# A hybrid encoder layer on one core: the mLSTM's backward pass copies its keys on DVE, loads its first decays earlier, and 36 projection products change place

## The chip, the cores and the metric

The kernel runs on one core of one Trainium2 chip. The metric is the device time of one execution in microseconds (us): the median of the runs of a kernel. Engines are named as in the profile: PE (TensorE), DVE (VectorE), ACT (ScalarE), POOL (GpSimd), SP (SyncE, which issues nearly all DMAs here).

## The reference, cut to what matters

One layer of a Hymba-style encoder over 2048 tokens of width 1024, in float32. After a modulated RMSNorm, one input projection feeds two groups of heads: eight attention heads of width 64 with two key/value heads in a band of 128 tokens, and four mLSTM heads of width 128, which scan the sequence forward and backward. Both groups are normalised, joined, projected and gated; a SwiGLU feed-forward layer and a last RMSNorm follow. The mLSTM of one head and direction, in chunks of 128 tokens:

```python
w = jnp.exp(a - a_max[..., None])
kv_c = jnp.einsum('bchs,bchsk,bchsv->bchkv', w, kc, vc)        # keys x weighted values, per chunk
c_new = decay[..., None, None] * c_st + inj[..., None, None] * kv   # state, chunk after chunk
sc = jnp.einsum('bchtd,bchsd->bchts', qc, kc) * dw              # scores in the chunk, with decays dw
num = (jnp.einsum('bchts,bchsv->bchtv', sc, vc)
       + inter[..., None] * jnp.einsum('bchtk,bchkv->bchtv', qc, c_prev))
hout = num / jnp.maximum(jnp.abs(den), jnp.exp(-m_t))[..., None]
```

Queries and keys of the mLSTM come from the projection through a convolution over three tokens and SiLU.

## The kernel before, in words

The order of PE's instructions is written out by hand for the whole kernel. In the mLSTM stage (from some 190 us to 572 us of the span) DVE, ACT, POOL and SP run in the order in which the code issues their work as well; from the attention on those four are ordered by a scheduler. PE works through the stage in order, so a product whose operand is late holds all that follows.

**Filler products.** Projection tiles are written as generators in the list `fill`; `pull(n)` issues the next n matmuls (`gps`, L607, 128x128 by 128x512, 96 for a tile of 128 columns by 2048 tokens, 24 for one block of 512). `at_step` runs between them what is due: a tile's weights are loaded (`wraw`, L257) and split in a high part on ACT (`whi`, L261) and a low part on POOL (`wlo`, L267), stores in `dues` are issued on SP (L296), and work in `posts` is run. After a block of a convolution tile ACT evicts it (L636, `edge` L637), DVE adds the neighbours (L641 and L642), later ACT takes the tanh (L622) and DVE multiplies (L625). While head h of the mLSTM runs, the tiles of the next head's queries and keys are its filler (768 products in all), and in the last head `first`, four tiles of attention keys and queries (384). The numbers of products in each place (`nb`, `nf`, `pull(5)`, `pull(36)`) are set by hand.

**One head of the mLSTM (`mlstm`)** has a backward pass over its 16 chunks, 15 to 0, and a forward pass. A chunk of the backward pass begins with `tick()`, which runs the work in `later` that is due. Then `k_chunk` transposes the chunk's keys on PE (`ktp`, L735, in PSUM bank a), copies them to SBUF (`kn`, L737, ACT), and scales the values (`vw`, L740, ACT). One chunk later PE multiplies the two (`kvp`, L745), and DVE brings the state on (`cb`, L766 for the first, L769 for the others). The sixteen `kn` of a head are kept, and the forward pass uses them again, except that of chunk 0, which it makes itself. `kvp` lies in banks c, d, c, b in turn. Keys and values are loaded in blocks of four chunks (`mqk`, `mv`); block 0 of queries, keys and values for the forward pass, and the decays `bc` of its first three chunks (L726), are loaded when the backward pass is at chunk 2.

The forward pass begins with `decays` (POOL, `ng`, L785), `scaled_q` (POOL, `qs`) and `exps` (ACT, L797). For each chunk PE then makes `sps` (L806, in banks d and b in turn), and for the chunk before it `kvp` (in bank a), and `num` (L836 and L838). DVE divides (`rd`, `hst`).

**The norm of a head** comes when its forward pass is over, so for heads 0 to 2 inside the next head's backward pass: 12 small instructions of DVE for the reciprocal square roots (L100 to L107), POOL scales four blocks (L867, `hst`), and `store` transposes each block on PE (`htp`, L872, bank a), scales it on ACT (`og`, L874, one buffer) and stores it by SP (L875, at the next tick). Blocks follow each other three ticks apart. Head 3's blocks are normalised one by one, the last in the tail: eight times a tick and `pull(5)`.

**The attention** starts with its loads `aq`, `ak`, `av` (L906 to L910), which read what `first` has stored, then `pull(36)` of its own filler (the tile `second` and the output-gate tiles), and the first scores `as` (L926). Its filler has 480 products; what the attention leaves of them is done at its end, around the start of the output projection (799 to 827 us).

Of the kernel before, what the change touches and what calls it, by code (L numbers as in the profile page):

```python
# [16 lines left out]
AF = mybir.ActivationFunctionType  # L17
# [5 lines left out]
P = 128  # L23
# [7 lines left out]
HM = 4  # L31
# [6 lines left out]
def hybrid_layer_kernel(  # L38
# [5 lines left out]
    pe, dve, act, pool, sp = nc.tensor, nc.vector, nc.scalar, nc.gpsimd, nc.sync  # L44
# [8 lines left out]
    def bank(tag, name):  # L53
        return pp.tile([P, 512], F32, tag=tag, name=name, bufs={"g": 2, "a": 2, "b": 1, "c": 2, "d": 1}[tag])
# [13 lines left out]
    mxm_d = dp.tile([HM, NT, P, P], F32, name="mxm_d")  # L68
# [43 lines left out]
    def pull(n=1):  # L112

        while n > 0 and fill:
            if next(fill[0], None) is None:
                fill.popleft()
            else:
                n -= 1

    def finish_fill(g):  # L120
        while any(f is g for f in fill):
            pull()
# [573 lines left out]
    later = []  # L696

    def tick():

        due = [f for k, f in later if k <= 0]  # L700
        later[:] = [[k - 1, f] for k, f in later if k > 0]
        for f in due:
            f()

    def load_v(h, n):
        va = s2.tile([P, 4, 129], F32, tag="mv", name="mv", bufs=2)
        sp.dma_start(va, vaug_d[n * 512:(n + 1) * 512, h, :].rearrange("(c p) d -> p c d", p=P))
        return va

    def load_qk(h, j, n):  # L710
        t = s2.tile([P, 512], F32, tag="mqk", name="mqk", bufs=4)
        sp.dma_start(t, qk_d[j, h, n])
        return t

    def load_last(h):
        return load_qk(h, 1, NB - 1), load_v(h, NB - 1)

    def mlstm(h, nb, nf, last):
# [5 lines left out]
        def load_bc(cc):  # L724
            bc = s2.tile([P, 4, P], F32, tag="bc", name="bc", bufs=3)
            sp.dma_start(bc.rearrange("p j t -> p (j t)"), bc_d[h, cc].rearrange("j t -> (j t)").partition_broadcast(P))  # L726
            return bc
# [3 lines left out]
        def k_chunk(k_c, va_c, d, cc):  # L731
            kn = kns.get(cc)
            if kn is None:
                tp = bank("a", "ktp")
                pe.transpose(tp[:, :P], k_c, ident)  # L735
                kn = kns[cc] = s2.tile([P, P], F32, tag=f"kn{cc}", name="kn", bufs=1)
                act.activation(kn, tp[:, :P], AF.Copy)  # L737
            vw = s2.tile([P, 129], F32, tag="vw", name="vw", bufs=3)
            rr = row(d, cc)
            act.activation(vw, va_c, AF.Copy, scale=wT[:, rr:rr + 1])  # L740
            return kn, vw

        def kv_mm(kn, vw, tag="a"):
            kvp = bank(tag, "kvp")
            pe.matmul(kvp[:, :129], kn, vw, start=True, stop=True)  # L745
            return kvp


        blk = {}
        todo = deque()  # L750
        blk[NB - 1] = last
        for cc in list(range(NT - 1, 0, -1)) + [0, 0]:
            tick()
            n, i = divmod(cc, 4)
            if i == 3 and n:
                blk[n - 1] = (load_qk(h, 1, n - 1), load_v(h, n - 1))
            if cc == 2:
                ahead = (load_qk(h, 0, 0), load_qk(h, 1, 0), load_v(h, 0)), [load_bc(i) for i in range(3)]
            if cc:
                todo.append((cc, *k_chunk(blk[n][0][:, i * P:(i + 1) * P], blk[n][1][:, i, :], 1, cc)))  # L760
                pull(nb - nb // 2)
            if len(todo) > 1 or (todo and not cc):
                c_, kn, vw = todo.popleft()
                kvp = kv_mm(kn, vw, "bcdc"[c_ % len("bcdc")])
                if c_ == NT - 1:
                    dve.tensor_copy(cb[:, c_ - 1, :], kvp[:, :129])  # L766
                else:
                    rr = row(1, c_)
                    dve.scalar_tensor_tensor(cb[:, c_ - 1, :], cb[:, c_, :], dec[:, rr:rr + 1], kvp[:, :129], MUL, ADD)  # L769
                pull(nb // 2)  # L770


        blk = {0: ahead[0]}
        out_ = []
        ssq = s2.tile([P, NT], F32, tag="mssq", name="mssq")
        ends = {NT - 1: 0} if h < HM - 1 else {4 * n + 3: n for n in range(NB)}
        bcs = dict(enumerate(ahead[1]))
        ngs, qss = {}, {}
        cf = None
        todo = None  # L780
# [18 lines left out]
        def scores(cc):  # L799
            n, i = divmod(cc, 4)  # L800
            if cc + 1 < NT:
                decays(cc + 1)
            qt, kt, va = blk[n]
            q_c, k_c, va_c = qt[:, i * P:(i + 1) * P], kt[:, i * P:(i + 1) * P], va[:, i, :]
            s = bank("db"[cc % 2], "sps")
            pe.matmul(s[:, :P], k_c, q_c, start=True, stop=True)  # L806
            kv = k_chunk(k_c, va_c, 0, cc) if cc < NT - 1 else None
            sc = s2.tile([P, 2, P], F32, tag="sc", name="sc")
            dve.scalar_tensor_tensor(sc, s[:, :P].unsqueeze(1).to_broadcast([P, 2, P]), DS, ngs.pop(cc), MUL, MUL)
            return cc, sc, va_c, kv  # L810
# [48 lines left out]
        def norm(n0, n):  # L859

            r = rsqrt(s2, ssq[:, 4 * n0:4 * n + 4], 4 * (n + 1 - n0), P, f"mr{n - n0}")
            for j in range(n0, n + 1):
                later.append([j - n0, partial(scale, j, r[:, 4 * (j - n0):4 * (j - n0) + 4])])
                later.append([3 * (j - n0) + 3, partial(store, j, out_[j])])
# [2 lines left out]
            pool.tensor_tensor(out_[j], out_[j], r.unsqueeze(2).to_broadcast([P, 4, P]), MUL)  # L867

        def store(n, hst):
            tp = bank("a", "htp")  # L870
            for i in range(4):
                pe.transpose(tp[:, i * P:(i + 1) * P], hst[:, i, :], ident)  # L872
            og = s2.tile([P, 512], F32, tag="og", name="og", bufs=1)
            act.activation(og, tp, AF.Copy, scale=gml[:, h:h + 1])  # L874
            later.append([0, lambda: sp.dma_start(mxm_d[h, 4 * n:4 * n + 4].rearrange("c p t -> p c t"),  # L875
                                                  og.rearrange("p (c t) -> p c t", c=4))])

        decays(0)
# [22 lines left out]
    def att_loads(bi, kv):  # L901
        k0, k1 = max(0, bi - 1), min(NT - 1, bi + 1)
        nk = k1 - k0 + 1
        ks = slice(k0 * P, (k1 + 1) * P)
        q = s3.tile([P, 4, P], F32R, tag="aq", name="aq")
        sp.dma_start(q.bitcast(F32), qst_d[kv * 4:kv * 4 + 4, :, bi * P:(bi + 1) * P].rearrange("h p t -> p h t"))  # L906
        kk = s3.tile([P, 2, 3 * P], F32R, tag="ak", name="ak")
        sp.dma_start(kk[:, :, :nk * P].bitcast(F32), kst_d[kv, :, :, ks].rearrange("z p t -> p z t"))
        v = s3.tile([P, 3, P], F32R, tag="av", name="av", bufs=4)
        sp.dma_start(v[:, :nk, :].bitcast(F32), vst_d[ks, kv].rearrange("(n p) z d -> p n (z d)", p=P))  # L910
        return bi, kv, nk, (k0 - bi + 1) * P, q, kk, v
# [211 lines left out]
    for i in range(2 * 96 + 60):  # L1123
# [8 lines left out]
        elif i == 226:  # L1132
            last = load_last(0)
# [5 lines left out]
    for h in range(HM):  # L1139
        if h:  # L1140
            for g in convs[h]:
                finish_fill(g)
            last = load_last(h)
            pull(45)
        mlstm(h, 3, 9, last)
    for _ in range(8):
        tick()
        pull(5)
    for g in first:
        finish_fill(g)  # L1150
    while posts:
# [148 lines left out]
    chain0 = first_pair(nxt)  # L1300
    order = [(bi, kv) for kv in range(KV) for bi in range(NT)]
    ahead = deque(att_loads(*o) for o in order[:2])
    pull(36)
    u1 = u2 = None
    for s_ in range(len(order) + 2):
        if s_ + 1 == NT:
# [414 lines left out]
    with tc.tile_pool(name="ff", bufs=1, side="right", reuse_waits="tile") as ff:  # L1721
# [203 lines left out]
        def operands(u, k):  # L1925
            if u == "A11":
                load_w2(W11, k)
            if u == "S2":
                load_w2(W22, k)
            a = load_a(u, k)  # L1930
            w = op_w(u, k)
            if u == "A11" :
                load_w2(W12, k)
            return a, w
# [106 lines left out]
        for u in ("A11", "S2", "S3", "A22", "S1", "S4", "A12"):  # L2041
# [11 lines left out]
            for k in range(KH - KL):  # L2053
                a, w = early.pop(0) if early else operands(u, k)
# [44 lines left out]
```

## Time and profile before

| | |
|---|---|
| median of 3 runs | 2274.69 us (2273.98 to 2275.52) |
| profiled execution | 2283.18 us, of which span 2281.4 us |
| PE busy | 2228.5 us, 98% of the span, 10968 matmuls |
| DVE, ACT, POOL busy | 1590.8 us, 1058.4 us, 1049.6 us |
| head 1: backward pass | about 318.5 to 338.3 us |
| head 2: backward pass | about 405 to 424 us |
| head 3: backward pass | about 492 to 510.5 us |
| start of the attention | from 571.7 us; its first scores at 587.31 us |

The profile is of one execution, whose own time is above the median of the runs. Times in rows are microseconds from the start of the span. In a row of the timeline the brackets at the end give how long the engine was idle before it, and what it then waited for. A row with x2 or more stands for as many instructions in a run, and its duration for all of them.

### The profile page before, as it was taken

What the parts mean: (1) busy time and instruction counts of PE and PEld (TensorE: products, weight loads), DVE (VectorE), ACT (ScalarE), POOL (GpSimd) and SP (SyncE); (2) the same over time, 40 slices, a digit from 0 to 9 for tenths busy, and PEclk for the clock granted to TensorE, in tenths of its full rate; (3) what the DMA queues carried; (4) which work ended last, traced back from release to release, by engine and by line L of the source; (5) the groups of instructions that cost most, each with busy time, mean ns of one, the idle gap of its engine ahead of it and who ended that gap; (6) DMA issues with size and microseconds to landing.
All of it is one profiled execution on the core that took longest, in us unless ns stands there. A gap on an engine that the chain in (4) does not pass through costs nothing.

```text
span 2281.4 us, 32599 instructions
## 1 busy us (share of the span) xinstructions
PE 2228.5 (98%) x10968; PEld 1875.9 (82%) x10968; DVE 1590.8 (70%) x2788; ACT 1058.4 (46%) x2204; POOL 1049.6 (46%) x909
## 2 busy tenths in 40 slices
PE   8999999999899999999999999999999999999998
PEld 8897878888788878778888888788888888888887
DVE  6876667546687887786767686776766666785694
ACT  5424655544577756354544443533333333233452
POOL 0007424425334434536656666456666655592020
PEclk9999999999999999999999999999999999999999
DMA  9667744776666576763343453533333373543462
GB/s 344 222 197 234 226 150 149 221 210 198 195 178 192 173 238 212 267 222 134 111 171 111 145 185 128 193 102 102 106 100 108 99 280 130 165 153 93 147 213 93
DMA packets 355500, 393.41 MB, mean 172 GB/s; under 512 B 21388, under 2 KB 253180, under 8 KB 355332
## 3 DMA queue, kind: packets, MB, share of 16 engines
q1 hardware_dynamic: 355108, 391.28, 52.6%
q8 instruction: 87, 1.43, 0.3%
q14 instruction: 81, 0.66, 0.1%
q10 hardware_dynamic: 224, 0.04, 0.0%
HBM read 272.05 MB, written 119.19 MB: 171 GB/s over the span
## 4 chain that ended last, share of the span: by engine, by line
PE 54%; DVE 2%; ACT 1%; DMA 1%; issue 1%; SPq 0%; ACTq 0%
PE fp L1747 36%; PE fo L59 5%; PE fo L58 5%; PE fo L57 5%; PE ops L57 1%; PE ops L59 1%; PE ops L58 1%; DVE al L1865 1%; DVE ra L2007 1%; DVE w L1874 0%; DMA al<-a_d 0%; ACT T L1561 0%; PE trn L167 0%; DMA A22r<-in_w_ffn_in_dram 0%; DVE ra L2023 0%
## 5 line engine op out<-in xcount | busy, mean ns | idle before, releaser
L607 PE MATMUL gps<-hT,whi 128*128 128x512 f32 x1088 | 398.4, 420 | 0.3 <-DVE cacc L642 0.3
L1747 PE MATMUL fp<-T,S 128*128 128x512 f32 x1584 | 368.9, 390 | 0.3 <-DVE T L1562 0.3
L1747 PEld LDWEIGHTS fp<-T,S 128*128 128x128 f32 x1584 | 296.4, 188 | 62.4 <-DVE T L1562 1.0
L1747 PE MATMUL fp<-B,A 128*128 128x512 f32 x1056 | 246.5, 389 | 0.0
L59 PE MATMUL fo<-w,al 128*128 128x512 f32 x616 | 239.8, 389 | 0.5 <-DVE al L1865 0.5
L58 PE MATMUL fo<-w,ah 128*128 128x512 f32 x616 | 239.7, 389 | 0.0
L57 PE MATMUL fo<-w,ah 128*128 128x512 f32 x616 | 239.7, 389 | 0.0
L1747 PEld LDWEIGHTS fp<-B,A 128*128 128x128 f32 x1056 | 198.2, 188 | 41.2
L607 PE MATMUL gps<-hT,wlo 128*128 128x512 f32 x544 | 227.7, 418 | 0.0
L607 PEld LDWEIGHTS gps<-hT,whi 128*128 128x128 f32 x1088 | 201.6, 191 | 24.0 <-DVE cacc L642 0.7
L1865 DVE TENSOR_TENSOR al<-al,ah 128x1024 fp32r<-128x1024 f32 x77 | 116.3, 1515 | 110.7 <-ACT ah L1864 110.1
L1864 ACT ACTIVATE ah<-al 128x1024 fp32r<-128x1024 f32 x77 | 81.6, 1060 | 183.5 <-DMA al<-a_d 182.2
L1597 DVE TENSOR_TENSOR S<-sf,S 128x512 fp32r<-128x512 f32 x86 | 132.4, 1577 | 30.0 <-ACT S L1596 29.9
L1597 DVE TENSOR_TENSOR A<-graw,A 128x512 fp32r<-128x512 f32 x86 | 132.7, 1565 | 11.2 <-ACT A L1596 11.1
L1767 DVE SCALAR_TENSOR_TENSOR g<-t,g 128x512 f32<-128x512 f32 x44 | 45.2, 1026 | 135.4 <-ACT t L1766 135.4
L59 PEld LDWEIGHTS fo<-w,al 128*128 128x128 f32 x616 | 115.6, 188 | 24.9 <-DVE al L1865 1.0
L58 PEld LDWEIGHTS fo<-w,ah 128*128 128x128 f32 x616 | 115.6, 188 | 24.2
L57 PEld LDWEIGHTS fo<-w,ah 128*128 128x128 f32 x616 | 115.6, 188 | 24.2 <-ACT ah L1864 0.2
L1747 PE MATMUL fp<-T,A 128*128 128x512 f32 x528 | 129.4, 394 | 2.1 <-ACT u L1773 2.1
L942 POOL TENSOR_SCALAR ap<-ap,adn 128x384 f32<-128x384 f32 (+1 forms) x128 | 73.0, 590 | 124.2 <-DVE adn L940 40.9
L1747 PE MATMUL fp<-B,S 128*128 128x512 f32 x528 | 127.0, 389 | 1.8 <-ACT c L1770 1.8
L1601 POOL TENSOR_TENSOR sf<-A,A22r 128x512 f32<-128x512 f32 x43 | 59.6, 1387 | 147.4 <-DMA A22r<-in_w_ffn_in_dram 104.0
(424 smaller groups left out, 5237.4 us busy)
## 6 DMA issues: line engine op xcount, KB each, us to landing
al<-a_d SPq DMA_DIRECT2D x77, 512.0 KB, 5.0
wmod<-in_w_mod_dram SPq DMA_DIRECT2D x48, 512.0 KB, 7.0
graw<-in_w_ffn_in_dram SPq DMA_DIRECT2D x43, 512.0 KB, 3.8
a_d<-ka SPq DMA_DIRECT2D x66, 256.0 KB, 4.5
bc<-bc_d SPq DMA_DIRECT2D x64, 256.0 KB, 4.7
hop_d<-n SPq DMA_DIRECT2D x56, 256.0 KB, 4.9
a_d<-u SPq DMA_DIRECT2D x55, 256.0 KB, 4.5
mqk<-qk_d SPq DMA_DIRECT2D x48, 256.0 KB, 4.1
```

Of the source, the lines that this page charges most:

```text
L57: pe.matmul(o, lh, rh, start=first, stop=False, skip_group_check=skip)
L58: pe.matmul(o, lh, rl, start=False, stop=False, skip_group_check=skip)
L59: pe.matmul(o, ll, rh, start=False, stop=last, skip_group_check=skip)
L607: pe.matmul(ps, w[i == 2][:, k, :], hT[n](i == 1, k), start=(k == 0 and i == 0), stop=(k == KT - 1 and i == 2))
L942: pool.tensor_scalar(self.p[g][:, :self.NK], self.p[g][:, :self.NK], dn[:, g:g + 1], 0.0, MUL, ADD)
L1597: dve.tensor_tensor(t[:, 1, :], f, t[:, 0, :].bitcast(F32), SUB)
L1601: pool.tensor_tensor(f1, a21, a22, ADD)
L1747: pe.matmul(ps, w[:, s, k * P:(k + 1) * P], f[k // 2][:, k % 2, :], start=first and n_ == 0, stop=n_ == 11, skip_group_check=True)
L1767: dve.scalar_tensor_tensor(g0, t0, 1.0, g0, ADD, MUL)
L1864: act.activation(ah, al.bitcast(F32), AF.Copy)
L1865: dve.tensor_tensor(al, al.bitcast(F32), ah.bitcast(F32), SUB)
L2007: dve.tensor_tensor(ra[i], ra[i], xr, ADD)
```

## The change

- In the backward pass the copy of the transposed keys, `kn`, is made by DVE in place of ACT (15 a head; the copy for chunk 0 in the forward pass stays on ACT).
- The decays of the first three chunks are loaded at chunk 8 of the backward pass, not at chunk 2; block 0 of the queries at chunk 5. Block 0 of keys and values is no longer loaded again for the forward pass: the buffers of the backward pass are used.
- The backward pass's `kvp` lie in banks c, d, c in turn (by the chunk's number modulo 3). The transposes `htp` of the results lie in bank b, except for head 3. The store of `og` is issued one tick later.
- The last head's forward pass pulls one filler product fewer at each of its 16 steps (nf 8 for 9), each of the eight steps of the tail 4 in place of 5, and 56 in place of 36 are pulled ahead of the attention's first scores. No product is added or dropped.

```diff
@@ k_chunk
-                act.activation(kn, tp[:, :P], AF.Copy)
+                if d:
+                    dve.tensor_copy(kn, tp[:, :P])
+                else:
+                    act.activation(kn, tp[:, :P], AF.Copy)
@@ mlstm, backward pass
-            if cc == 2:
-                ahead = (load_qk(h, 0, 0), load_qk(h, 1, 0), load_v(h, 0)), [load_bc(i) for i in range(3)]
+            if cc == 8:
+                bcs = {i: load_bc(i) for i in range(3)}
+            if cc == 5:
+                q0 = load_qk(h, 0, 0)
...
-                kvp = kv_mm(kn, vw, "bcdc"[c_ % len("bcdc")])
+                kvp = kv_mm(kn, vw, "cdc"[c_ % 3])
...
-        blk = {0: ahead[0]}
+        blk = {0: (q0, *blk[0])}
...
-        bcs = dict(enumerate(ahead[1]))
@@ store
-            tp = bank("a", "htp")
+            tp = bank("b" if h < HM - 1 else "a", "htp")
...
-            later.append([0, lambda: sp.dma_start(mxm_d[h, 4 * n:4 * n + 4].rearrange("c p t -> p c t"),
+            later.append([1, lambda: sp.dma_start(mxm_d[h, 4 * n:4 * n + 4].rearrange("c p t -> p c t"),
@@ the heads, the tail, the attention
-        mlstm(h, 3, 9, last)
+        mlstm(h, 3, 9 if h < HM - 1 else 8, last)
     for _ in range(8):
         tick()
-        pull(5)
+        pull(4)
...
-    pull(36)
+    pull(56)
```

## Rows read from the trace of the kernel before

**Rows 1.** The page, first part: busy time, share of the span, instructions.
```profile
PE 2228.5 (98%) x10968; PEld 1875.9 (82%) x10968; DVE 1590.8 (70%) x2788; ACT 1058.4 (46%) x2204; POOL 1049.6 (46%) x909
```

**Rows 2.** Waits of PE, 230 to 660 us: us in total, times, longest.
```profile
PE kvp L745 <- ACT vw L740: 7.3, 8, 2.3
...
PE ktp L735 <- ACT og L874: 2.3, 3, 1.3
...
PE sps L806 <- DVE cb L769: 0.5, 1, 0.5
```

**Rows 3.** Windows: length, busy PE, PEld, DVE, ACT, POOL, granted clock, DMA, GB/s.
```profile
200.00:220.00 20.00, 20.00 (x90) 16.57 (x89) 1.00 0.85 284
...
430.00:433.00 3.00, 3.00 (x9) 2.41 (x8) 2.86 (x10) 2.70 (x10) 1.40 (x2) 0.50 0.97 296
586.60:593.40 6.80, 6.09 (x18) 5.18 (x19) 3.01 (x13) 2.50 (x9) 0.92 (x3) 0.50 0.79 241
799.00:827.00 28.00, 26.73 (x124) 21.92 (x123) 23.69 (x45) 15.02 (x20) 9.96 (x8) 1.00 0.89 296
```

**Rows 4.** Timeline at the turns of heads 1, 2 and 3: start, us, instruction.
```profile
335.70 0.50 SPq L726 DMA_DIRECT2D bc<-bc_d  x1
...
341.20 0.74 POOL L785 TENSOR_TENSOR ng<-bc,maskb 128x256 f32<-128x256 f32 x1 [13.93 <-DMA bc<-bc_d]
...
343.17 0.49 PE L745 MATMUL kvp<-vw,kn 128*128 128x129 f32 x2 [1.33 <-ACT vw L740]
...
428.19 0.49 PE L745 MATMUL kvp<-vw,kn 128*128 128x129 f32 x2 [2.05 <-ACT vw L740]
...
515.73 0.49 PE L745 MATMUL kvp<-vw,kn 128*128 128x129 f32 x2 [2.26 <-ACT vw L740]
```

**Rows 5.** Instructions by form: ns least/median/most, first and last start.
```profile
L737 ACT ACTIVATE kn<-ktp x64: 252/277/287, 236.0 to 515.1; 128x128 f32<-128x128 f32 x64
L766 DVE COPY cb<-kvp x4: 278/288/292, 237.4 to 492.3; 128x129 f32<-128x129 f32 x4
L625 DVE SCALAR_TENSOR_TENSOR cacc<-ctanh,cacc x32: 679/692/1783, 193.6 to 433.4; 128x512 f32<-128x512 f32 x32
```

**Rows 6.** Timeline of DVE, then PE, start of head 1's backward pass.
```profile
320.00 0.16 DVE L100 TENSOR_SCALAR mr3v<-mssq 128x16 f32<-128x16 f32 x1
...
322.08 0.17 DVE L107 SCALAR_TENSOR_TENSOR mr3y<-mr3a,mr3y 128x16 f32<-128x16 f32 x1
...
322.38 3.00 DVE L625 SCALAR_TENSOR_TENSOR cacc<-ctanh,cacc 128x512 f32<-128x512 f32 x2
...
323.43 0.38 PE L745 MATMUL kvp<-vw,kn 128*128 128x129 f32 x2
```

**Rows 7.** Timeline of PE, start of head 3's backward pass.
```profile
490.69 0.28 PE L735 MATMUL ktp<-ident,mqk 128*128 128x128 f32 x1
...
492.87 0.38 PE L745 MATMUL kvp<-vw,kn 128*128 128x129 f32 x2
```

**Rows 8.** Timeline: head 2's start on DVE; head 1's turn on PE, DVE.
```profile
406.29 0.75 DVE L641 SCALAR_TENSOR_TENSOR cacc<-gps,cvw,cacc 128x511 f32<-128x511 f32 x1 [2.24 <-ACT edge L637]
...
338.35 0.38 PE L806 MATMUL sps<-mqk 128*128 128x128 f32 x2
...
340.02 0.34 DVE L769 SCALAR_TENSOR_TENSOR cb<-cb,dec,kvp 128x129 f32<-128x129 f32 x1
```

**Rows 9.** Timeline: og in head 3; PE and SP from tail to attention.
```profile
504.66 0.69 ACT L874 ACTIVATE og<-htp,gml 128x512 f32<-128x512 f32 x1 [2.36 <-DMA mxm_d<-og]
...
573.38 0.66 PE L872 MATMUL htp<-ident,hst 128*128 128x128 f32 x4 [1.64 <-POOL hst L867]
...
576.12 0.38 SPq L257 DMA_DIRECT2D wraw<-in_w_in_dram  x1
...
583.39 0.50 SPq L908 DMA_DIRECT2D ak<-kst_d  x1
...
587.31 0.55 PE L926 MATMUL as<-ak,aq 128*128 128x256 f32 x1 [5.08 <-DMA ak<-kst_d]
```

## The prediction

> **What bounds the kernel now.** I read the page's first part, then the waits of PE over the mLSTM and the start of attention, then the stretches around each wait. PE is busy for 98% of the span [rows 1], so a change pays only where it removes idle time of PE or work that PE has to repeat at a low clock. Nothing here removes a product: the projection products are moved, not dropped. What can be had is therefore the list of PE's waits between 230 and 660 us, of which the change touches 16.8: 7.3 on vw, 2.3 on og, 0.5 on cb [rows 2], 1.64 on the last normalised outputs and 5.08 on the first attention keys [rows 9]. To that come stretches in which the granted clock is 0.50 [rows 3]. PE's order is written out, so a wait of PE in one place is not made good by later work; it adds to the end. The same holds in this stage for what DVE, ACT, POOL and SP have queued, each in program order.
>
> **First decays loaded at chunk 8.** The three big vw waits stand at the turns from the backward to the forward pass of heads 1 to 3: 1.33, 2.05 and 2.26 us [rows 4], 5.64 together. The chain is in the rows of head 1: the bc load is issued at 335.70, POOL's ng starts at 341.20 when it has landed, the exps come behind it on ACT and vw behind these, and kvp starts at 343.17. Issued six chunks earlier, at some 1.15 us for a chunk (the 16 of head 1's backward pass lie between 320.00 and 338.35 [rows 6, 8]), the load lands about 7 us before it is needed. −5.64. The kept first keys drop two loads a head from SP's queue just where the q load and the bc loads are issued; nothing waits for those two, 0.
>
> **Keys copied by DVE.** The copy itself costs the same: 277 ns on ACT, and a copy of 128x129 from PSUM takes 288 ns on DVE [rows 5]. The Trainium skill's page "Perfetto Trace Analysis", section "Optimizing Scalar/DVE Operations", speaks against the move: it gives the overhead of one access to PSUM as about 125 ns for DVE and 51 for Scalar. By that the copies would be 74 ns longer each, an estimated 0.7 us over the ten or so that stand on PE's path; the two rows differ by 11 ns, so I count nothing for it.
>
> What costs is the place in DVE's queue. kn is now behind whatever DVE has in program order, and kvp, which has no other work of PE ahead of it to hide in, waits. I set DVE's order out by hand from the code and gave each instruction its traced duration.
>
> - *The square root of the norm.* In heads 1 to 3 the norm of the head before puts 12 small instructions between kn of chunk 15 and kn of chunk 14, from 320.00 to 322.25, 2.25 us [rows 6]. In head 3 the transpose starts at 490.69 and the product of chunk 14's keys is started 2.18 later [rows 7]. With DVE: 0.28 + 0.29 + 2.25 + 0.29 and some 0.14 of hand-overs = 3.25. +1.07 in head 3, and the same inside heads 1 and 2.
> - *Head 1.* There kn 14 would be done for a product at 323.07. Then come cb (0.29), kn 13 (0.28), two L625 that take 3.00 together [rows 6] because POOL works beside them (the median of one is 692 ns [rows 5]), cb (0.35) and kn 12 (0.28): 327.4 with hand-overs for a product that started at 323.43 [rows 6]. +4.0.
> - *Head 2.* L641 (406.29, 0.75 us) and L642 behind it stand ahead of kn 13 [rows 8]: beyond the 1.07 another 1.0. +2.06.
> - *Evictions of projection tiles elsewhere.* Each L641 and L642 pair holds DVE for 1.5 us plus its wait for ACT, while kvp is due some 2.2 us after its transpose. By the same sum: head 0 twice (+1.13, +1.15), head 1 +0.6, head 2 +0.6.
>
> Together 4.0 + 2.06 + 1.07 + 1.13 + 1.15 + 0.6 + 0.6 = 10.6. From below the copies could cost nothing, if DVE stands idle whenever one comes, and even give something, since ACT is freed of 60 x 0.277 us in a stage where vw waits behind it; from above each head could pay what head 1 does, 16, and the evictions 3.5. I take the sums, which are the only values worked out from the rows of these places.
>
> **Banks c and d, transposes in bank b, store one chunk later.** With three banks in turn, the kvp of chunk 1 lies in d, and the first scores, also in d, wait for cb of chunk 1 rather than of chunk 2. In head 1 that cb starts at 340.02, behind L641 and L642, and the scores started at 338.35 [rows 8]: +1.8 with what og adds there. Heads 2 and 3: +0.6 and +0.2; head 0: −0.2, since its wait of 0.5 is there already [rows 2]. The transposes no longer wait for og in bank a (2.3 us of ktp [rows 2]). But ACT still stops at og until the store before has landed: 504.66, after 2.36 us of waiting [rows 9]. With the store one chunk later that wait is no shorter, and vw is behind it on ACT, so kvp takes over the wait of ktp. From −2.3 to +1; I take −0.6, in head 3, the rest nil.
>
> The heads by themselves: head 0 +2.1; head 1 4.0 + 0.6 + 1.8 − 1.33 = +5.1; head 2 2.06 + 0.6 + 0.6 − 2.05 = +1.2; head 3 1.07 + 0.2 − 0.6 − 2.26 = −1.6. Sum +6.8.
>
> **More products at the end.** Head 3's forward pass gives up 16 products, which are done in the tail, and 20 of the attention's are done before its first scores. Products follow each other at 20.00/90 = 0.222 us [rows 3]. Before, the last of the first projections ended at 573.38 − 1.64 = 571.74, then PE waited 1.64 for hst and 5.08 for ak [rows 9]. In the tail the 16 cover the 1.64; the 20 take 4.4 us ahead of the scores. The keys hang on SP: a weight load is issued at 576.12, the stores of queries behind it, ak only at 583.39 [rows 9]; the scores start at 587.31, 15.6 us after that end. After: PE arrives 56 x 0.222 = 12.4 us after it, the keys at about 15.2 (the tail's chain on hst is shorter by some 0.4), so 2.8 of 6.72 is left. −3.9, and +0.2 for head 3's forward pass, where there is less to cover DVE. −3.7 (from −6.7, if SP isn't blocked, to −1, if the keys move with the last product). The same 20 are missing at the end of attention, 799 to 827, where DVE is busy 23.69 of 28 us [rows 3] and the output projection waits for it: from 0 to +4.5, I take +0.5.
>
> **Clock.** The stretch at 430 to 433 (3.00 us, clock 0.50 [rows 3]) follows the wait of 2.05, and goes with it: −1.5. The stretch after the keys (586.6 to 593.4) stays, with 2.8 us of waiting ahead of it. From −4.5 (both go) to +3 (two new ones of 1.5).
>
> **Sum.** 6.8 − 3.7 + 0.5 − 1.5 = +2.1. The durations come from one execution of 2283.18 us (span 2281.4, 1.8 around it), 8.5 above the median of 2274.69; the excess lies in no stage that I could name, so I carry over the difference: 2285.3 there, 2276.8 for the median. That is within 0.2% (4.5 us) of before, about what a measurement of this kernel can tell from no change.
>
> **Rivals.**
> - *DVE finds room.* The copies cost half or less: PE, delayed once, is late everywhere after, so that the next kvp is no longer early. For it: DVE is not the bound in these stretches, and waits that I added one by one may overlap. Against it: head 1's 3.00 us pair. The waits that I add in the heads are 13.0 and those taken away 6.2; from 6.4 of added ones downward the whole is faster by more than 4.5. With a third of 13.0 (4.3), og's 2.3 gone (in place of 0.6), and the start as above: −5.64 − 2.3 + 4.3 − 3.7 + 0.5 − 1.5 = −8.3, 2266.4. Chance 0.36.
> - *The backlog lowers the clock (the slower side).* Head 1's two waits of some 2 us stand close together. One of 2.05 was followed by 0.50 at 430; against it, one of 2.26 at 515.73 was not, nor the 1.33. If heads 0 and 1 get two such stretches and the one at 430 stays: 6.8 − 3.7 + 0.5 + 3.0 = +6.6, 2281.3. It decides from a single wait of about 2 us on DVE in head 1. Chance 0.20.
> - *Moving the products doesn't do what it says.* If the keys' load hangs on the last product of the first projections, what is moved ahead of it moves the load too, and the start gives −1 only: 2279.5. For it: SP's weight load at 576.12 waits for POOL, which follows the last products. Chance 0.10.
>
> **Numbers.** Forecast 0.34, 2276.8, its own range 2271 to 2280. The third rival lies just past the bound of 4.5: 0.07 of it counts as slower, 0.03 as the same. Faster by over 0.2%: 0.36. Within: 0.34 + 0.03 = 0.37. Slower: 0.20 + 0.07 = 0.27. Range: down to 2264 (the first rival with og's wait and the clock's full −4.5), up to 2284 (the second with the end of attention at +3).
>
> **What would show it.** After the change: no wait of kvp for ng or vw at the three turns; new waits of kvp for DVE's kn in heads 1 and 2, the largest near chunk 12 of head 1, about 2 us; sps waiting for cb at the turn of head 1; as waiting about 2.8 us for ak, and the SP order before it unchanged. The forecast is wrong if kvp's waits for kn sum to under 6 us, if as waits not at all or still 5 us, or if 799 to 827 grows by more than 2 us.

## The result, and the profile after

The change made the kernel slower: 2289.24 us median of 5 runs (2285.54 to 2294.34) against 2275.52 of before (2273.98 to 2280.11), a ratio of 1.0057 with a 95% interval of 1.0038 to 1.0075. A second set on another chip, where before has 2281.4, gave 2290.16 and 1.0036 (1.0023 to 1.0050). The profiled execution of the changed kernel was its quickest, 2285.54 us (span 2283.7), and that of before one of its slower ones (2283.18), so the two profiles differ by 2 us only. What they are good for is the stages. The table takes them from the timeline's first instructions: backward pass from the head's first ktp to its first sps; forward pass from there to the next head's first ktp, in head 3 to the first `as`, tail included; attention from there to the first ops; output projection to its last ops, at about 1000 us. "Again" is the profile of the second set.

| us | before | after | again |
|---|---|---|---|
| backward passes, heads 0 to 3 | 17.6, 19.8, 18.6, 19.3 | 18.9, 26.4, 24.0, 25.0 | 18.8, 27.6, 23.9, 24.9 |
| forward passes, heads 0 to 3 | 65.3, 65.7, 68.0, 77.3 | 65.3, 65.8, 64.3, 72.3 | 65.3, 65.8, 64.3, 72.3 |
| attention | 239.5 | 232.6 | 234.8 |
| output projection | 173.7 | 176.2 | 180.5 |

The backward passes lose 19 to 20 us. All the rest wins 13.0 in the first profile and 6.5 in the second, so that the stages of the table together take 6.0 and 13.4 us longer than in the one profile of before; by the ratios the change costs 13 and 8 us. (20 products, 4.4 us, went from the attention's row to that of head 3; the sum of both is free of that.)

First the page's busy times, then PE's waits from 230 to 660 us in the changed kernel (us in total, times, longest), which answer to [rows 1] and [rows 2].

```profile
PE 2230.6 (98%) x10968; PEld 1877.1 (82%) x10968; DVE 1599.2 (70%) x2848; ACT 1045.7 (46%) x2144; POOL 1051.6 (46%) x909
```

```profile
PE kvp L748 <- ACT vw L743: 8.3, 5, 2.5
PE kvp L748 <- DVE kn L738: 5.4, 7, 1.1
PE sps L810 <- DVE cb L774: 2.9, 4, 2.3
PE ktp L735 <- DMA mqk<-qk_d: 0.9, 1, 0.9
...
PE kvp L748 <- DVE mr3v L100: 0.6, 1, 0.6
```

The waits of ktp for og are gone, and so are those for hst and for the first attention keys. But vw still costs 8.3 us, in fewer and longer waits. The timeline of head 1 shows that these are not the waits of [rows 4], which stood at the turn, but new ones ahead of it; the last two rows are those of heads 2 and 3.

```profile
328.93 1.47 SPq L726 DMA_DIRECT2D bc<-bc_d  x3
330.45 0.43 SPq L712 DMA_DIRECT2D mqk<-qk_d  x1
330.97 0.38 SPq L707 DMA_DIRECT2D mv<-vaug_d  x1
332.08 0.37 SPq L879 DMA_DIRECT2D mxm_d<-og  x1
...
338.10 0.69 ACT L878 ACTIVATE og<-htp,gml 128x512 f32<-128x512 f32 x1 [5.04 <-DMA mxm_d<-og]
...
339.13 0.49 PE L748 MATMUL kvp<-vw,kn 128*128 128x129 f32 x2 [1.85 <-ACT vw L743]
...
429.62 0.38 PE L748 MATMUL kvp<-vw,kn 128*128 128x129 f32 x1 [1.88 <-ACT vw L743]
...
518.83 0.38 PE L748 MATMUL kvp<-vw,kn 128*128 128x129 f32 x1 [2.50 <-ACT vw L743]
```

Read from the top: SP issues the early decay loads, then the next block of keys and values, and only then the store of og. ACT, which has the next block to write into the one og buffer, stands idle for 5.04 us until that store has landed, and writes 6.0 us after the store's issue. vw is behind og in ACT's order, and kvp, which needs vw, is next in PE's.

The windows (length, busy PE, PEld, DVE, ACT, POOL, granted clock, DMA share, GB/s) answer to [rows 3]:

```profile
328.00:336.00 8.00, 7.71 (x49) 6.39 (x47) 5.25 (x15) 3.87 (x10) 0.73 (x1) 1.00 0.95 266
345.30:348.70 3.40, 3.29 (x9) 2.79 (x10) 0.48 (x2) 2.24 (x7) 0.73 (x1) 0.50 0.87 296
430.60:434.00 3.40, 3.40 (x15) 2.92 (x13) 0.83 (x3) 1.17 (x3) 0.76 (x2) 0.51 0.34 118
519.30:522.70 3.40, 3.40 (x14) 2.96 (x13) 1.59 (x5) 0.80 (x3) 1.29 (x2) 0.52 0.60 156
799.00:830.00 31.00, 28.38 (x133) 22.80 (x132) 23.91 (x47) 17.86 (x24) 9.99 (x9) 1.00 0.82 271
830.00:833.40 3.40, 3.40 (x12) 2.81 (x11) 3.40 (x5) 2.88 (x6) 0.97 (x1) 0.50 0.70 200
```

The DMA engines are busy for 0.95 of 328 to 336. Of the four waits of 1.85 us and more between 230 and 660 us, three are followed by 3.4 us at a clock of about 0.50, which is at most 1.7 us lost each (half of 3.4): that of sps at 345.41 (next fence but one), and those of kvp at 429.62 and 518.83. The one at 339.13 is not.

The key copies on DVE, by form (ns least, median, most), and what stands around them at the start and the turn of head 1, for [rows 5, 6, 8]:

```profile
L738 DVE COPY kn<-ktp x60: 277/291/293, 235.3 to 522.6; 128x128 f32<-128x128 f32 x60
```

```profile
320.88 0.46 PE L748 MATMUL kvp<-vw,kn 128*128 128x129 f32 x2 [0.57 <-DVE mr3v L100]
...
323.25 0.46 PE L748 MATMUL kvp<-vw,kn 128*128 128x129 f32 x2 [1.10 <-DVE kn L738]
...
326.63 0.46 PE L748 MATMUL kvp<-vw,kn 128*128 128x129 f32 x2 [1.07 <-DVE kn L738]
...
344.35 0.75 DVE L642 SCALAR_TENSOR_TENSOR cacc<-gps,cvw,cacc 128x511 f32<-128x511 f32 x1 [0.46 <-DVE cacc L641]
345.02 0.34 DVE L774 SCALAR_TENSOR_TENSOR cb<-cb,dec,kvp 128x129 f32<-128x129 f32 x1
...
345.41 0.80 PE L810 MATMUL sps<-mqk 128*128 128x128 f32 x2 [2.25 <-DVE cb L774]
```

The start of the attention, for [rows 9], and its end:

```profile
589.87 0.50 SPq L912 DMA_DIRECT2D ak<-kst_d  x1
...
596.68 0.28 PE L930 MATMUL as<-ak,aq 128*128 128x256 f32 x1
...
829.33 0.50 PE L57 MATMUL ops<-wo,mA 128*128 128x512 f32 x1 [2.52 <-ACT oth L692]
```

The keys are asked for 6.8 us ahead of the scores and PE doesn't wait at all, where in [rows 9] it waited 5.08 us for them and 1.64 for the last normalised outputs. At the other end the output projection waits 2.52 for oth; before, that wait was 1.26. Behind it the clock is 0.50 for 3.4 us (last row of the windows), which is most of the 2.5 us that the output projection takes longer.

### The profile page after: what moved, and what is told of

Same layout as the page of the kernel before. It is cut to its first block, busy times and chain, and to the rows that moved or that the text cites. A ratio compares the mean times of both kernels' runs of the same rounds, so it can differ in the third digit from the quotient of the medians.

```text
span 2283.7 us, 32593 instructions
## 1 busy us (share of the span) xinstructions
PE 2230.6 (98%) x10968; PEld 1877.1 (82%) x10968; DVE 1599.2 (70%) x2848; ACT 1045.7 (46%) x2144; POOL 1051.6 (46%) x909
## 4 chain that ended last, share of the span: by engine, by line
PE 54%; DVE 2%; ACT 1%; DMA 1%; issue 1%; SPq 0%; ACTq 0%
PE fp L1751 36%; PE fo L59 5%; PE fo L57 5%; PE fo L58 5%; PE ops L57 1%; PE ops L58 1%; PE ops L59 1%; DVE al L1869 1%; DVE ra L2011 1%; DMA al<-a_d 0%; DVE w L1878 0%; ACT T L1565 0%; PE trn L167 0%; DMA A22r<-in_w_ffn_in_dram 0%; DVE ra L2027 0%
## 5 line engine op out<-in xcount | busy, mean ns | idle before, releaser
L57 PEld LDWEIGHTS fo<-w,ah 128*128 128x128 f32 x616 | 115.6, 188 | 23.9 <-ACT ah L1868 0.3
```

The lines of the kernel that those rows point to most:

```text
L57: pe.matmul(o, lh, rh, start=first, stop=False, skip_group_check=skip)
```

## The experiments

Each ran beside the kernel before, on one chip for each set of kernels, so times are compared by their ratio to before's in the same set (its medians are 2278.12 us beside e1 to e4, 2279.84 beside e5 to e8, 2281.39 beside e9 to e12, and 2278.72 beside e13 and e14). A thousandth is 2.3 us.

Theory L (landing): the early decay loads make the store of og land late, ACT waits, vw behind it. Theory K: the key copies wait in DVE's order. Rivals stand with each run.

**e1: og written over the block that was transposed,** so that no og waits for a store.

```diff
-            og = s2.tile([P, 512], F32, tag="og", name="og", bufs=1)
+            og = hst.rearrange("p c t -> p (c t)")
```

> The changed kernel with og written into the hst tile that was just transposed, so that no store waits in front of the next og. Theory L (landing): ACT waits for the og buffer until the store before has landed, 5.0, 3.1 and 5.9 us in the changed kernel, vw behind it, and kvp waits 1.85, 1.88 and 2.50 near chunk 3 of heads 1 to 3; each of these is followed by 3.4 us at clock 0.50 (1.7 us lost). All three go: 6.2 + 5.1 = 11.3 us less than the changed kernel's 2289.2, about 2278. Rival K (key copies behind DVE's queue): those waits are only where an unavoidable delay shows, kvp's waits for kn (5.4) and sps' for cb (2.9) grow by what vw's lose, and the time stays at 2287 or more.

2279.47, ratio 1.0002 (0.9994 to 1.0011): 8 to 13 us under the change (1.0036 and 1.0057). kvp's waits for vw went from 8.3 to 1.3, those for kn stayed:

```profile
PE kvp L748 <- DVE kn L738: 4.4, 5, 1.1
PE sps L810 <- DVE cb L774: 2.9, 4, 2.3
PE ktp L735 <- DMA mqk<-qk_d: 2.3, 3, 1.0
PE kvp L748 <- ACT vw L743: 1.3, 1, 1.3
```

So ACT's wait for the store is what costs this, as theory L has it. K's form, that other waits would grow by as much, falls: against the 7.0 that vw's lost, ktp's for mqk grew by 1.4 and one of 0.8 (kvp for ctanh) is new.

**e2: the decay loads back at chunk 2**, all else of the change kept.

```diff
-            if cc == 8:
+            if cc == 2:
                 bcs = {i: load_bc(i) for i in range(3)}
```

> The changed kernel with the first three bc loads at chunk 2 again. Theory L in the form that the early bc loads fill the DMA queues in front of the og store: the store lands in 2 to 4 us instead of 6, the waits of kvp near chunk 3 fall from 6.2 to under 2, and the turns wait again for ng (about 5.6 us, or more): about as the changed kernel, 2285 to 2290. Rival D (the store's delay by one tick is enough by itself): the waits near chunk 3 stay at 5 to 6 and the turns' come on top, 2294 or more.

2278.39, ratio 0.9997 (0.9987 to 1.0006). The og landing is relieved as L has it, but I had expected the waits of the turns to come back, and they did not: vw costs 2.5 us in all. So the early loads cost 9 to 14 us of the change (from 1.0036 and 1.0057) and gave nothing that the rest did not give. e12 says what gave it.

**e3: the store issued at the next tick again.**

```diff
-            later.append([1, lambda: sp.dma_start(mxm_d...
+            later.append([0, lambda: sp.dma_start(mxm_d...
```

> The changed kernel with the store of og issued at the next tick again (delay 0). Rival D: the store goes one chunk (1.0 to 1.5 us) earlier and lands that much earlier, the three waits near chunk 3 shrink from 6.2 to some 2 to 3 and at least two of the low-clock stretches go: 2281 to 2284. Theory L with the bc loads as the cause: the DMA engines are busy to 336 whatever the order, the store lands at the same time to within 0.5 us, and the time stays at 2287 to 2290.

2291.33, ratio 1.0051 (1.0038 to 1.0064): no change. The three waits near chunk 3 are still there, with 1.84, 1.87 and 2.27 us. The delay is not the cause.

**e4: the key copies on ACT again.**

```diff
-                if d:
-                    dve.tensor_copy(kn, tp[:, :P])
-                else:
-                    act.activation(kn, tp[:, :P], AF.Copy)
+                act.activation(kn, tp[:, :P], AF.Copy)
```

> The changed kernel with the key copies on ACT again. Rival K: kvp's waits for kn and for the square root (5.4 + 0.6) go, and the turn of head 1, where sps waits 2.25 for a cb behind L641 and L642, stays: about 6 to 8 us less, 2281 to 2283. Theory L: the kn copies then stand behind the blocked og on ACT as well, the waits near chunk 3 stay or grow (ktp of the next chunk too), and 3 us at most are gained: 2286 to 2289.

2280.64, ratio 1.0008 (0.9998 to 1.0017), as K has it. Its one profile is of an execution of 2286.03, above all its others, and still shows vw waits of 8.9 us; what the other executions had in their place isn't seen.

**e5: both undone**, copies on ACT and loads at chunk 2.

> The changed kernel with the key copies on ACT and the bc loads at chunk 2; the kept first keys, the early q load, the banks, the store's delay and the moved products stay. Theory L + K (the early bc loads cost some 11 us by the og landing, the copies on DVE some 8): both go, and what the moved products give (some 10 us net) is left: 2268 to 2272 where the kernel before has 2278. The backward passes are then 17.6, 20, 19 and 20 us. Rival O (both only let the same late vw show, so that undoing either gives all there is): 2277 to 2280. For the turns: if the two reloads of keys and values were what delayed bc, kvp waits under 0.7 us there; if not, 1.3 to 2.3 each again.

2272.28, ratio 0.9964 (0.9952 to 0.9976): both prices are real and add up. From e5, the early loads cost 0.0044 (e4), the copies 0.0033 (e2); together 1.0041, inside what the change has. Head 1's backward pass takes 23.1 us where 20 was expected: vw still waits 1.48 us behind og in it, and sps 1.9 for cb.

**e6: the kernel before with the three decay loads at chunk 8**, nothing else.

```diff
+            if cc == 8:
+                bc0 = [load_bc(i) for i in range(3)]
             if cc == 2:
-                ahead = (...), [load_bc(i) for i in range(3)]
+                ahead = (...), bc0
```

> The kernel before with its first three bc loads at chunk 8 and nothing else. Theory L: the turns' waits (5.6 us) go, but the og stores land late, ACT waits 3 to 6 us for og in heads 1 to 3, and ktp or kvp waits 1.8 to 2.5 near chunk 3 in each: between -1 and +4 us, the backward passes of heads 1 to 3 some 2 to 5 us longer, the forward ones 2 to 4 shorter. My prediction's own step (early load gives -5.6, and no price): 2270 to 2273 on this chip's 2278.

2287.78, ratio 1.0033 (1.0021 to 1.0045): 7.5 us slower, more than theory L gave it. PE's waits from 230 to 660, then ACT's:

```profile
PE ktp L735 <- ACT og L876: 12.1, 4, 4.8
...
PE kvp L745 <- ACT vw L740: 0.9, 3, 0.4
```

```profile
ACT og L876 <- DMA mxm_d<-og: 14.8, 4, 5.8
```

In stages: the forward passes 8.4 us shorter (65.3, 64.1, 64.2, 74.3), since the turns' waits are gone; the backward ones 15.9 longer (17.9, 24.7, 23.6, 25.0). The prediction had the first of these and not the second. Not all of the 15.9 is waiting. PE's waits for og grew by 9.8 (12.1 for the 2.3 of [rows 2]), and in these backward passes the granted clock is 0.50 for 17.0 us, where before has no such stretch in its own. PE is busy for 14.5 of them, so by an estimate some 7 us are lost to the clock (windows as above):

```profile
340.30:343.70 3.40, 3.40 (x15) 2.84 (x14) 0.70 (x2) 0.75 (x3) 0.87 (x2) 0.50 0.93 300
425.60:432.40 6.80, 5.75 (x19) 4.89 (x20) 0.70 (x2) 2.99 (x9) 2.10 (x3) 0.50 0.66 193
514.40:521.20 6.80, 5.38 (x18) 4.56 (x19) 1.39 (x3) 2.99 (x9) 1.91 (x3) 0.50 0.64 189
```

**e7: the kernel before with the key copies on DVE**, nothing else.

> The kernel before with the key copies on DVE and nothing else. Theory K: kvp waits for kn and the square root in heads 0 to 3, 5 to 6 us, and sps at head 1's turn: the backward passes grow by 1.2, 4.2, 1.7 and 1.3 us, the whole by 7 to 9: 2285 to 2287. Rival (the copies cost only beside the early bc loads, since ACT is free enough without them): +0 to +3.

2285.20, ratio 1.0025 (1.0016 to 1.0034): 5.7 us slower, less than expected, and not only beside the early loads. The backward passes grew by 0.8, 2.3, 1.8 and 0.2.

**e8: the kernel before with the moved products**, nothing else.

> The kernel before with the moved products alone (8 for 9 in the last head, 4 for 5 in the tail, 56 for 36 ahead of the attention). The profile of the changed kernel has head 3's forward pass to the first scores 5.0 shorter with 20 more products in it, and the stretch from there to the output projection 6.9 shorter with 20 fewer; its head 3 also lost the 2.26 of the turn, which stays here: as waits under 0.5 for ak, htp not at all, ops waits 2.5 in place of 1.3 for oth at the end of the attention. -6 to -9: 2269 to 2272. Rival (the keys' load moves with the last product, my third): -1 to -2.

2275.00, ratio 0.9980 (0.9969 to 0.9990): 4.6 us faster, under the 6 to 9 expected. Neither htp nor as waits any more; but at the end of the attention ops waits 2.7 for oth and 1.4 for mA, and 3.4 us at half clock follow. Another 3.4 us at half clock came earlier in the attention, behind a wait of ao for apth of 2.1 us (before 1.35).

**e9: e5 with og written over its block** (the edits of e1, e2 and e4).

> As e5 (key copies on ACT, bc loads at chunk 2, the rest of the change), and og written into hst. e5 has 1.48 and 0.74 in head 1 and 1.79 in head 3 left on vw behind og. Theory L: these go, 2 to 4 us less than e5, 0.9945 to 0.9955 of before. Rival (single og buffer costs nothing once bc is late): as e5, 0.996 to 0.997.

2268.97, ratio 0.9948 (0.9934 to 0.9962). kvp's waits for vw fall from 5.7 in e5 to 2.4, so the og buffer makes PE wait also where the loads are late. The time is 0.0016 under e5's, but the two ran on different chips and their intervals overlap. What is left in head 1 is sps waiting 1.9 for cb.

**e10: the kernel before with the kept first keys, q at chunk 5, the moved products and og over its block**; banks, the store's tick, the key copies and the decay loads as before.

> The kernel before with first keys and values kept, q at chunk 5, the moved products, and og written into hst; banks, the store's tick, kn on ACT and bc at chunk 2 as before. If the new banks cost the wait of sps for cb at head 1's turn (1.9 in e5) and give nothing, it is 1 to 2 us under e9; if htp's own bank gives what ktp waits for og (2.3 before), it is level with e9 or 2 above. Either way 2268 to 2273 for before's 2279.

2265.93, ratio 0.9931 (0.9919 to 0.9944): the best of all, 15.5 us under before, and better than the range expected. Every wait of PE from 230 to 660 us, and that stretch as a window:

```profile
PE kvp L745 <- ACT vw L740: 1.5, 5, 0.4
PE num L839 <- DVE rd L845: 0.8, 1, 0.8
PE sps L807 <- DVE cb L771: 0.5, 1, 0.5
PE ktp L735 <- DMA mqk<-qk_d: 0.4, 1, 0.4
```

```profile
230.00:660.00 430.00, 426.49 (x2454) 367.13 (x2453) 282.91 (x893) 253.90 (x775) 179.55 (x254) 1.00 0.65 194
```

With og over its block, the new banks and the store's delay seem worth nothing: e9 has them and is 0.0017 slower (the intervals overlap), with sps waiting 1.9 us for cb at head 1's turn and 3.4 us at a clock of 0.50 there.

**e11: the change once more.**

> The changed kernel once more, for a second profile and beside the same runs of before as the next ones. Theory L + K: 10 to 14 over before; ACT waits 3 to 6 for og once in each of heads 1 to 3, kvp 1.8 to 2.5 behind it, and the backward passes of heads 1 to 3 are 5 to 7 us over before's, as in the first profile, since they follow from the order of the queues. Rival (a chance of single executions): other places.

2290.16, ratio 1.0036; its stages stand above. The waits near chunk 3 came in the same places: 1.86, 1.90 and 2.59 us.

**e12: the kernel before with the first keys and values kept and q loaded at chunk 5**, the decays still at chunk 2.

```diff
             if cc == 2:
-                ahead = (load_qk(h, 0, 0), load_qk(h, 1, 0), load_v(h, 0)), [load_bc(i) for i in range(3)]
+                bcs = {i: load_bc(i) for i in range(3)}
+            if cc == 5:
+                q0 = load_qk(h, 0, 0)
```

> The kernel before with block 0's keys and values kept and q loaded at chunk 5; bc still at chunk 2. If the three loads in front of bc (q, k, v of block 0) were what made it land late at the turns: the waits of 1.33, 2.05 and 2.26 fall under 0.7 each with the clock's stretch after them, 4 to 7 us less than before. My prediction's step (nothing waits for those loads): no change, within 1 us.

2273.53, ratio 0.9965 (0.9952 to 0.9979): 8 us faster, a little more than expected. The forward passes are 65.3, 64.1, 64.1 and 74.7, as in e6, and kvp waits 1.6 for vw in all, where [rows 2] has 7.3:

```profile
PE kvp L745 <- ACT vw L740: 1.6, 5, 0.6
```

Without three loads in front of them the decays are issued 4.2 us ahead of head 1's first sps (336.48 and 340.65), where they had 2.65 (335.70 and 338.35), and ng starts 0.5 after that sps, not 2.85. What the two dropped loads and the moved q give by themselves was not run.

**e13: the kernel before with one decay load of three at chunk 8**, the other two at chunk 2.

> The kernel before with only the first of the three bc loads at chunk 8, the other two at chunk 2. Theory L, bytes form (the og store lands late because three loads of 256 KB and the two key and value loads stand ahead of it in the transfer queues): with one in place of three, some 1.5 us less traffic an extra load, ACT's longest wait for og falls from 5.8 to 3 to 4.5 and PE's ktp waits for og from 12.1 (e6) to 4 to 8; the turn waits go as in e6, since ng needs the first load only: -2 to +3. Rival (any load at chunk 8 upsets SP's order against the store): as e6, +6 to +9.

2278.09, ratio 0.9996 (0.9987 to 1.0005), as expected: ACT's longest wait for og falls from 5.8 to 3.4, PE's waits for og from 12.1 to 4.5.

```profile
PE ktp L735 <- ACT og L876: 4.5, 3, 2.4
...
PE kvp L745 <- ACT vw L740: 1.4, 5, 0.3
```

The turns' waits are gone with the first load alone. So the price goes with the number of the loads, and not with the mere fact that something is loaded at chunk 8.

**e14: e10 with the three decay loads at chunk 8.**

> As e10 (kept first keys, products moved, og in hst, on the kernel before), with the three bc loads at chunk 8. Theory L (the landing of og's store is the only price of the early loads): level with e10, -1 to +2, 0.993 to 0.994. Rival (the early loads also hold up the block loads of keys, mqk): ktp waits 2 to 4 us more for mqk, 3 to 5 over e10, 0.9945 or more.

2268.84, ratio 0.9955 (0.9943 to 0.9968): 5.5 us over e10 by the ratios, whose intervals only touch (the two ran on different chips), and the rival was right. With no og to wait for, the early loads hold up the next block's keys instead:

```profile
PE ktp L735 <- DMA mqk<-qk_d: 5.2, 3, 2.2
PE kvp L745 <- ACT vw L740: 1.9, 6, 0.4
```

So theory L in its narrow form (the store of og is the only victim) falls: the block of keys, which stands behind the three loads too, is late as well. The Trainium skill's page "DMA: Bandwidth & Descriptors", section "Queues, rings and completion order", says that an issuing engine's transfers share one ring on each DMA engine and that descriptors are consumed there in ring order. e6, e13 and e14 agree: the store and the keys are late by the loads issued ahead of them.

## Why the prediction was wrong, step by step

Two terms were put at nothing without a look at the queue. What the early decay loads hold up cost 15.9 us in e6's backward passes, and what keeping the first keys, with q moved, gives was 8.0 (e12). By its own signs the forecast is wrong twice: kvp's waits for kn sum to 5.4, under 6, and as does not wait.

- **First decays loaded at chunk 8: −5.64, no price.** The gain was sized well: with the clock's 1.5 it was to be 7.1, and e6's forward passes gained 8.4. The step failed in its price: three loads of 256 KB were put ahead of the store of og and of a block of keys, and nothing was reckoned for it. That costs 15.9 in e6's backward passes, 9.8 of it in waits for og and much of the rest in the low clock that follows them. The prediction told of the moved loads only when they would land, and not what is queued behind them. (The 7 us in it are how much earlier than in [rows 4] the load lands; there it came 1.33 us too late, so it lands 5 to 6 us before it is needed.)
- **Kept first keys: "nothing waits for those two, 0".** Wrong by 8 us the other way (e12, which moves q as the change does). The three loads stood ahead of bc, whose landing ended the turns' waits; the chain of [rows 4] was followed back to the issue of bc, but not to what was in the queue before it. Since this part alone takes the turns' waits away (vw costs 1.6 in e12, and 2.5 in e2, where the decays are late again), the early loads had nothing left to give, and only their price stayed.
- **og: "that wait is no shorter"**, kvp takes over the wait of ktp. The mechanism was right and named; the term was −0.6, from a row of 2.36 us of the kernel before [rows 9]. After, it is 5.04 in head 1 and 5.9 in head 3, since the early loads now stand ahead of the store; the prediction did not connect the two.
- **Key copies in DVE's order, 10.6.** Right in place and mechanism, too large: the rows after have 0.57 + 1.10 + 1.07 in head 1 for my 4.0, and kn and the square root together cost 5.4 + 0.6. L625's pair took 2.60 us, not 3.00; that a late kvp leaves the next one less to wait, as the first rival has it, fits but was not tested by itself. Alone the part costs 5.7 (e7), from e5 to e2 7.5. The copy itself takes 291 ns, 14 more than on ACT. The 74 more, an estimate from the overheads that the Trainium skill's page "Perfetto Trace Analysis" ("Optimizing Scalar/DVE Operations") gives, are not seen in these durations.
- **sps waiting for cb of chunk 1 at head 1's turn, +1.8.** Measured 2.25; what was missed is the 3.4 us at half clock behind it.
- **Start of the attention: 2.8 of 6.72 left.** Nothing is left; that is the best case the text gave (−6.7). SP's order did not stay. Counted back 56 products, 12.4 us, from the scores at 596.68, the first projections end at 584.2 and ak is issued 5.6 us behind that end; before, it was 11.65 (571.74 and 583.39). **End, +0.5:** the wait for oth grew by 1.3, and the output projection by 2.5 and 6.8 in the two profiles, mostly at a low clock. Alone the moved products give 4.6 (e8), for the forecast's 3.2. The rival that moving them does nothing was wrong.
- **Clock, −1.5.** Over all runs it went the other way. The mean granted clock over the span is 0.9944 and 0.9937 in the two sets of the change, and 0.996 for before beside the experiments. At half speed a stretch loses half its length, so a mean lower by 0.002 is by an estimate some 4.5 us lost, a third to a half of the whole. The first profile, of the quickest execution, does not show it between 230 and 660 us: three stretches of 3.4 us came, and before's two, of 3.4 and 6.8 us, went, the longer one with the wait for ak.

The second rival (a backlog that lowers the clock, 2281.3, chance 0.20) had the sign and half the cause: new waits of about 2 us, three of them followed by a low clock. But it put them on DVE in head 1; two of the three stand on ACT, behind a store.

Put together from the parts alone: 7.5 (e6) + 5.7 (e7) − 4.6 (e8) − 8.0 (e12) + 4.3 = 4.9. The 4.3 is a remainder, e5's 0.9964 less the gains of e8 and e12; it stands for the banks and the store's tick, which no run has alone on the kernel before. The gain at the turns is counted in both e6 and e12 and can be had once; added back, the 8.4 of e6's profile, this gives 13.3, for the 13 and 8 that were measured. With a remainder and a single profile in it, this is weaker than the sum under e5, which has runs alone in it and gives 9.3 us (1.0041).

What stays open: what the banks do by themselves; what the other executions of e4 had in place of the waits in its profile; and why the change's ratio differs by 0.002 between two chips, with intervals that overlap.

## What to carry to other kernels

A load that is issued earlier is ahead of other transfers: list what is issued in the next few microseconds on the same queue, and who waits for its landing, before booking the gain. When a wait ends with a load's landing, look first at what stands in front of that load; to drop two such loads and move a third was worth 8 us here, to move the load itself cost 7.5. A single staging buffer put the next instruction that fills it, and all behind that on its engine, behind a store's landing; where the source tile is dead, write over it.

## What the runs showed of the hardware that was not expected

A store of og (256 KB) issued 3.2 us after the first of three loads of the same size, with a block of keys and values between, let its buffer go 6.0 us after its issue, with the DMA engines busy for 0.95 of 328 to 336 us. A single wait of PE of about 2 us was enough for the clock to go to half: in the changed kernel 3.4 us at 0.50 after waits of 2.25, 1.88 and 2.50; before, 2.05 did and 2.26 did not; and in e5 one of 1.90 did not. So in these rows the length of the wait does not settle it. In e10, which has no wait over 0.8 us from 230 to 660, the granted clock stays at 1.00 there.
